# A hybrid attention and state-space layer: the first column blocks turned by diagonal products, a seventh accumulator, joined convolution taps, closing products in one order

## The chip, the cores and the metric

The kernel runs on one NeuronCore of one Trainium2 chip. The metric is device time in microseconds (us) of one execution; the kernel before takes 942.23 us, the median of three runs.

## The reference

One layer over 512 latent tokens and 256 context tokens of width 1024. Both are root-mean-square normalised row by row, shifted and scaled by modulation vectors, and multiplied by one input projection. Its columns feed a low-rank attention with 16 heads, a state-space scan over `x`, `B` and `C` after a depthwise convolution of width 5, and a gate `z`. An output projection, a second modulated norm and a gated feed-forward layer of inner width 2816 follow. Cut to what the change touches:

```python
hx = modulate(rms_norm(x, mix_pre_norm), mod_x[0], mod_x[1])       # 512 x 1024
cq_x, ckv_x, kr_x, z_x, xbc_x, dt_x = in_split(hx @ w_in)
hc = modulate(rms_norm(ctx, mix_pre_norm), mod_c[0], mod_c[1])     # 256 x 1024
xbc = silu(depthwise_conv(xbc, conv_w, conv_b))                    # latent and context apart
ssd = rms_norm(y * silu(z), norm_w)
x = x + mod_x[2] * rms_norm(concat([attn, ssd]) @ w_out, mix_post_norm)
ffn = (gelu(depthwise_conv(gate)) * val) @ w_down
x = x + mod_x[5] * rms_norm(ffn, ffn_post_norm)
```

Everything is float32.

## The kernel before, in words

**How a product is made.** Each operand is split into a high part in float32r and the remainder (`split`: ScalarE copies the high part, VectorE subtracts). A product is three float32r matmuls: high by high, high by low, low by high. Tiles are 128 rows; the 1024 columns are 8 blocks of 128, counted by `k`.

**The start.** SyncE loads four row tiles of `x` (`xn`), two modulation columns and the parameters, then for each `k` the 128 rows of the `z` weights (two halves of 512 columns) and two more modulation columns. PE first runs products of zeros (`IDLE`, 22 of them), then eight small products that spread the vector `c` over all partitions into PSUM (`spread`), then 20 more products of zeros. `unit_rows` squares and sums each row on ScalarE, makes 1/root on VectorE and GpSimd (`rsqrt`: a power on GpSimd, then one Newton step on VectorE), and multiplies each 1024-wide row tile by it (odd tiles on ScalarE, even ones on VectorE); it is called once for tiles 0 and 1 and once for tiles 2 and 3. `columns_of` turns two column blocks of two row tiles by four PE transposes into one PSUM bank, and ScalarE copies them out. `moddot` makes one modulation column by a 1024-wide dot product on VectorE; `factors` makes shift and scale from two of them; `modulated` writes the high part `hx[k]` and the full value on ScalarE, and VectorE makes the low part. Then `part_of_z` multiplies.

**z.** There are eight output tiles of 128 tokens by 512 columns, numbered `n`: 0 to 3 are the first half of the columns, 4 to 7 the second. Each needs a PSUM bank while it sums over `k`. Tiles 0 to 3 hold banks 0 to 3 from `k` = 0. Banks 4 and 5 serve `columns_of`, 6 the products of zeros, 7 is kept free (`m`); tiles 4 to 7 get these four (line 855).

**The x, B and C blocks.** `xbc(m)` makes one block of 128 channels: 24 products over the latent tokens into columns 0 to 511 of a two-bank piece, 24 over the context into columns 512 to 767, then the convolution: ScalarE writes the middle tap with the bias, and VectorE adds the four other taps, once for the latent and once for the context columns.

**The closing.** The down projection is made of seven half-size products in two `series`. The first sums eight accumulators (`n` = 0 to 3, `i` = 0 and 1), the second six (`n` = 0 to 2). In each, the last few `k` of every accumulator (3 and 4 of them) are kept back, and `pins` make the accumulators close one after the other in a given order. After each one `done` adds it to sums on VectorE; an accumulator of the second series needs the sums of the first (`summed_last` reads `u3`, `u2`, `p1`), and when a row tile is whole, `last` normalises it, adds `x` and stores it.

**What sets the order.** The program is written once in plain order; `plan` then orders every engine's instructions by a list scheduler with its own costs (`price`), seeded by `SEED`, with `pins` as extra dependences. Where the instructions of an engine stand is therefore a result of all costs together. All recorded instructions carry the line L137 in the profile, so groups are read by their tiles: `banks` is PSUM, `block` any SBUF tile, `smalls` the per-row scalars.

## Time and profile before

| what | value |
|---|---|
| median of three runs | 942.23 us (941.97 to 942.94) |
| the profiled execution's own time | 942.26 us |
| its span, first to last instruction | 940.5 us |
| PE busy | 917.8 us |
| VectorE (DVE) busy | 808.0 us |
| ScalarE (ACT) busy | 558.6 us |
| GpSimd (POOL) busy | 244.6 us |
| mean granted TensorE clock | 0.992 |

The span plus 1.76 us is the profiled execution's time, and that time is 0.03 us above the median. A row of the timeline gives the start, the length, the engine, the operation with its tiles and shape, and in brackets how long the engine stood idle before it and what ended that. A row of a table by stretch gives the length of the stretch, then for each engine the busy time and the number of instructions, the granted clock, the DMA share and the GB/s. Some matmul records are missing from the trace, so time per product is better taken from starts over a known count.

### The profile page before, as it was taken

The page shows a single profiled execution, that of the slowest core. Times are in us where ns is not written, and L with a number is a line of the kernel's source. Part 1 is how long each engine was busy: PE and PEld are TensorE (multiplying, and loading weights), DVE is VectorE, ACT ScalarE, POOL GpSimd, SP SyncE. Part 2 cuts the span into 40 slices and gives each one's busy share as a digit, 9 for nine tenths or more (in the row PEclk, how much of TensorE's full clock was granted, in tenths as well). Part 3 has the DMA queues.
Part 4 walks back from the last instruction along what each step waited for, and adds up shares of the span by engine and source line. Part 5 has one row for each costly group of instructions (what it writes and reads, how often), then busy time and mean ns, then how long its engine had stood idle before and what let it go on. Part 6 is the DMA issues. An engine that isn't in the chain of part 4 may idle for free.

```text
span 940.5 us, 15221 instructions
## 1 busy us (share of the span) xinstructions
PE 917.8 (98%) x5382; PEld 793.5 (84%) x5382; DVE 808.0 (86%) x1362; ACT 558.6 (59%) x1091; POOL 244.6 (26%) x240
## 2 busy tenths in 40 slices
PE   7999999999999999999999999999999999999994
PEld 6888888788778887988888888899999998888883
DVE  5899887759888988789999828799999899999976
ACT  7667535375668798887875317654454454556631
POOL 1000200847684643610000001600000355330200
PEclk8999999999999999999999999999999999999998
DMA  9999101011521450566639527315243235358732
GB/s 364 348 372 357 35 34 46 7 52 40 122 65 35 125 151 25 157 184 173 197 137 355 187 106 238 121 68 174 73 135 113 68 135 170 124 189 275 194 113 90
DMA packets 51068, 139.97 MB, mean 149 GB/s; under 512 B 8608, under 2 KB 11632, under 8 KB 50992
## 3 DMA queue, kind: packets, MB, share of 16 engines
q1 hardware_dynamic: 48448, 137.85, 44.7%
q10 hardware_dynamic: 2544, 1.15, 0.5%
q8 instruction: 42, 0.69, 0.3%
q14 instruction: 34, 0.28, 0.1%
HBM read 113.90 MB, written 9.35 MB: 131 GB/s over the span
## 4 chain that ended last, share of the span: by engine, by line
PE 84%; DVE 6%; ACT 3%; issue 3%; DMA 2%; POOL 1%; DVEq 0%; POOLq 0%; SPq 0%; ACTq 0%
PE banks L137 84%; DVE block L137 5%; ACT block L137 3%; DVE smalls L137 2%; DMA block<-block 1%; POOL smalls L137 1%; DMA block<-shares 1%; DMA block<-in_xn_dram 1%; POOL block L137 0%; DVEq L1867 0%; POOLq L1867 0%; SPq L137 0%; ACTq L137 0%; DVEq L137 0%; DVE mod L137 0%
## 5 line engine op out<-in xcount | busy, mean ns | idle before, releaser
L137 PE MATMUL banks<-block,block 128*128 128x512 f32 (+2 forms) x4662 | 867.8, 344 | 4.0 <-DVE block L137 1.4
L137 PEld LDWEIGHTS banks<-block,block 128*128 128x128 f32 x4662 | 713.3, 189 | 109.6 <-issue 12.8
L137 DVE TENSOR_TENSOR block<-block,block 128x512 fp32r<-128x512 f32 (+7 forms) x459 | 351.0, 800 | 43.5 <-PE banks L137 16.7
L137 ACT ACTIVATE block<-block 128x512 fp32r<-128x512 f32 (+9 forms) x399 | 267.6, 707 | 202.3 <-DVE block L137 121.5
L137 POOL TENSOR_TENSOR block<-block,block 128x512 f32<-128x512 f32 (+2 forms) x145 | 176.1, 1231 | 312.4 <-DVE block L137 138.5
L137 DVE TENSOR_TENSOR block<-banks,block 128x512 f32<-128x512 f32 (+5 forms) x287 | 168.4, 609 | 33.8 <-PE banks L137 19.1
L137 ACT ACTIVATE block<-banks 128x512 fp32r<-128x512 f32 (+6 forms) x276 | 135.9, 514 | 77.1 <-PE banks L137 68.5
L137 POOL TENSOR_TENSOR block<-block 128x256 f32<-128x256 f32 (+1 forms) x51 | 48.4, 953 | 187.5 <-PE banks L137 132.4
L137 PE MATMUL banks<-cst,block 128*128 128x128 f32 x562 | 89.0, 276 | 3.5 <-DVE block L137 1.8
L137 DVE SCALAR_TENSOR_TENSOR block<-block,block 128x1024 f32<-128x1024 f32 (+2 forms) x74 | 86.9, 1190 | 2.4 <-ACT block L137 1.6
L137 PEld LDWEIGHTS banks<-cst,block 128*128 128x128 f32 x562 | 68.4, 142 | 19.4 <-issue 4.2
L137 ACT ACTIVATE block<-banks,smalls 128x768 f32<-128x768 f32 x64 | 58.0, 907 | 21.2 <-DVE smalls L137 20.5
L137 DVE TENSOR_REDUCE smalls<-banks 128x1 f32<-128x768 f32 x64 | 60.7, 949 | 7.8 <-PE banks L137 6.3
L137 DVE SCALAR_TENSOR_TENSOR block<-banks,cwh,block 128x510 f32<-128x510 f32 (+3 forms) x88 | 52.0, 621 | 7.5 <-ACT block L137 6.9
L137 POOL TENSOR_TENSOR smalls<-smalls,powers 128x1 f32<-128x1 f32 (+3 forms) x17 | 13.0, 767 | 165.1 <-DVE smalls L137 165.1
L137 ACT ACTIVATE block<-banks,block 128x128 f32<-128x128 f32 x128 | 42.2, 382 | 10.7 <-PE banks L137 10.4
L137 ACT ACTIVATE block<-banks,cbh,cwh 128x512 f32<-128x512 f32 (+1 forms) x22 | 14.8, 684 | 26.4 <-PE banks L137 25.6
L137 DVE TENSOR_TENSOR block<-block 128x512 f32<-128x512 f32 (+2 forms) x30 | 20.2, 675 | 1.7 <-DMA block<-in_wup_dram 1.5
L137 ACT ACTIVATE block<-banks,prm 128x512 f32<-128x512 f32 x18 | 13.3, 738 | 9.1 <-PE banks L137 8.1
L137 DVE TENSOR_SCALAR smalls<-smalls 128x1 f32<-128x1 f32 (+3 forms) x36 | 5.9, 170 | 13.1 <-ACT block L137 12.8
L137 ACT ACTIVATE block<-block,prm 128x512 f32<-128x512 f32 x12 | 9.8, 814 | 11.8 <-DVE block L137 11.8
L137 ACT ACTIVATE block<-block,mod,sx 128x512 fp32r<-128x512 f32 (+1 forms) x16 | 13.1, 817 | 4.5 <-DVE sx L137 4.2
(72 smaller groups left out, 234.2 us busy)
## 6 DMA issues: line engine op xcount, KB each, us to landing
block<-in_wmod_dram SPq DMA_DIRECT2D x64, 512.0 KB
block<-in_wup_dram SPq DMA_DIRECT2D x44, 512.0 KB
block<-in_wdn_dram SPq DMA_DIRECT2D x22, 512.0 KB
block<-block SPq DMA_DIRECT2D x32, 256.0 KB
block<-in_wout_dram SPq DMA_DIRECT2D x16, 512.0 KB
block<-block SPq DMA_DIRECT2D x56, 128.0 KB
block<-in_wxbc_dram SPq DMA_DIRECT2D x12, 512.0 KB
block<-in_xn_dram SPq DMA_DIRECT2D x8, 512.0 KB
```

Source lines behind the costliest of these rows:

```text
L137: f(*map(real, args), **{k: real(v) for k, v in kw.items()})
```

## The change

1. **Turning.** For the first two column blocks (`k` = 0 and 1), `columns_of` no longer transposes scaled rows. It multiplies the unscaled block by a 128 by 128 diagonal of 1/root, which turns and scales at once; the diagonals are made on VectorE. The rows are scaled later (`scaled_rows`), for the other blocks. The two modulation columns of `k` = 0 are written ahead of the second pair of rows, and `modulated` works in two halves of 256 tokens for `k` = 0 and 1.
2. **Products of zeros.** The second lot is 34 instead of 20.
3. **Banks.** `spread` uses banks 6 and 7, `columns_of` one bank (4) instead of two; z tiles 4, 5 and 6 hold banks 5, 6 and 7 from `k` = 0, and the eighth tile takes bank 4 at the end.
4. **Taps.** In `xbc` the context columns start at 514, two columns of zeros (written by ScalarE into PSUM) lie between, and each tap is one operation over latent and context columns.
5. **Closing.** `series` returns its last closing, and the second series' first closing is pinned behind the first series' last one.
6. **Planner and loads.** `SEED` is 4 instead of 2, a GpSimd operation on under 8 elements is priced at 550 ns, and the constants are loaded first on SyncE's queue instead of second on ScalarE's. `Calls` records source lines, which changes no instruction.

```diff
-SEED = 2
+SEED = 4
-IDLE = 22, 20
+IDLE = 22, 34
+FM = 2
...
+    if e == "Pool" and n < 8:
+        return 550
...
-    bk.cut(a=[two(0), two(2)], b=[bank(4), bank(5)], s=[bank(6)], m=[bank(7)])
+    bk.cut(a=[two(0), two(2)], b=[bank(4)], s=[bank(5)], v=[two(6)])
...
-    load(cst, a["cst"][:, : P + 32], nc.scalar)
+    load(cst, a["cst"][:, : P + 32])
...
-    def columns_of(pair, k, to):
+    def columns_of(pair, k, to, turn=None):
...
+                if turn is None:
+                    nc.tensor.transpose(o, src, ident)
+                else:
+                    mm(o, lhsT=src, rhs=turn[:, i * P : (i + 1) * P], start=True, stop=True)
...
-    unit_rows(xn[:2])
-    unit_rows(xn[2:])
+    turns = []
+    for h in range(2):
+        pair, turn = xn[2 * h : 2 * h + 2], t2(P, 256)
+        r = unit_rows(pair)
+        for i in range(2):
+            V.tensor_scalar(out=turn[:, i * P : (i + 1) * P], in0=ident, scalar1=r[:, i : i + 1], scalar2=None, op0=ALU.mult)
+        columns_of(pair, 0, xT[0][:, :, h * 256 : h * 256 + 256], turn)
+        turns.append(r)
+        if not h:
+            scaled_rows(pair, r)
+            for j in (0, KD)[:FM]:
+                moddot(wmods[j], pv, mod[:, j : j + 1])
...
+        if k == 1:
+            scaled_rows(xn[2:], turns[1])
-        if k % 2 == 0:
+        if k and k % 2 == 0:
...
+            bk.cut(v=[], s=[bank(5), bank(6), bank(7)])
+            zp += [pget("s") for _ in range(3)]
...
+    zp.append(pget("b"))
...
+        n = CO + CT if m < 10 else S
+        if m < 10:
+            act(pm[:, S:CO], none, AF.Copy)
+        gemm_T(blk(w), KD, ((pm[:, :S], hxv), (pm[:, CO:n], hcv))[: 2 if m < 10 else 1])
+        st = t4(P, n)
+        act(st, pm[:, :n], AF.Identity, scale=cwh[:, m * 5 + 2 : m * 5 + 3], bias=cbh[:, m : m + 1])
...
-    def series(terms, banks, keep, done, order):
+    def series(terms, banks, keep, done, order, after=None):
...
-        at = []
+        at = [after] if after else []
...
+        return at[-1]
...
-    series(rest_of_right, banks(3), 4, summed_last, [(n, i) for n in range(3) for i in range(2)])
+    series(rest_of_right, banks(3), 4, summed_last, [(n, i) for n in range(3) for i in range(2)], first_done)
```

**Where instructions move.** PE at the start of the program, before. `128x256` are the products of zeros, `sel` the spread, `cst` the identity of a transpose, `block_2` to `block_5` the row tiles 0 to 3, `128x512` the first products of z.

```order
L137 MATMUL banks<-block_1_87 128x256 x22
L137 MATMUL banks<-block_1_87,sel 128x128 x8
L137 MATMUL banks<-block_1_87 128x256 x19
L137 MATMUL banks<-cst,block_2_85 128x128
...
L137 MATMUL banks<-cst,block_4_98 128x128
L137 MATMUL banks<-cst,block_5_107 128x128
...
L137 MATMUL banks<-block_1_87,block_20_231 128x512
```

The same place after the change; `block_16_175` and `block_21_224` are the diagonals of the two pairs of row tiles.

```order
L688 MATMUL banks<-block_1_87 128x256 x22
L688 MATMUL banks<-block_1_87,sel 128x128 x8
L688 MATMUL banks<-block_1_87 128x256 x21
L688 MATMUL banks<-block_16_175,block_2_91 128x128
...
L688 MATMUL banks<-block_1_87 128x256 x13
L688 MATMUL banks<-block_21_224,block_4_101 128x128
...
L688 MATMUL banks<-block_1_87,block_24_222 128x512 x2
```

Before, 20 transposes (column blocks 0 to 3 of tiles 0 and 1, then blocks 0 and 1 and so on) stand ahead of the first product of z and 12 between its first products; after, 8 products by diagonals stand ahead of it, with 13 products of zeros between the first four and the last four, and the 24 other transposes stand among the products of z, in sixes of four.

VectorE at the same place, before: `block_2_85` and `block_4_98` are row tiles 0 and 2, `block_6` and `block_7` the modulation columns.

```order
L137 SCALAR_TENSOR_TENSOR smalls<-smalls 128x2
L137 TENSOR_SCALAR block_2_85<-block_2_85,smalls 128x1024
L137 TENSOR_SCALAR smalls<-smalls 128x2 x2
L137 TENSOR_TENSOR smalls<-smalls 128x2 x2
...
L137 TENSOR_SCALAR block_4_98<-block_4_98,smalls 128x1024
L137 SCALAR_TENSOR_TENSOR block_16_125,mod<-block_6_119,banks 128x1024
L137 SCALAR_TENSOR_TENSOR block_22_211,mod<-block_7_131,banks 128x1024
L137 TENSOR_TENSOR mod<-mod,prm 128x2
L137 SCALAR_TENSOR_TENSOR sx<-mod,prm 128x1
```

After, from the first pair's 1/root on.

```order
L688 TENSOR_SCALAR block_16_175<-cst,smalls 128x128 x2
L688 TENSOR_SCALAR block_2_91<-block_2_91,smalls 128x1024
L688 SCALAR_TENSOR_TENSOR block_19_195,mod<-block_6_124,banks 128x1024
L688 TENSOR_SCALAR smalls<-smalls 128x2
L688 SCALAR_TENSOR_TENSOR block_20_208,mod<-block_7_134,banks 128x1024
...
L688 TENSOR_TENSOR smalls<-smalls 128x2
L688 TENSOR_TENSOR mod<-mod,prm 128x2
...
L688 SCALAR_TENSOR_TENSOR sx<-mod,prm 128x1
L688 SCALAR_TENSOR_TENSOR smalls<-smalls 128x2
L688 TENSOR_SCALAR block_21_224<-cst,smalls 128x128 x2
```

The two dot products now stand ahead of the second pair's 1/root, and the second pair's diagonals come after `sx`, the scale factor of `k` = 0.

PE at the end of the program, before: the last products. `block_1236` and `block_1240` are left operands of the first series, `block_1478` and `block_1488` of the second; each group of three rows is one `k` of one accumulator.

```order
L137 MATMUL banks<-block_1511_8571,block_1236_7788 128x512
L137 MATMUL banks<-block_464_2860,block_1236_7788 128x512
L137 MATMUL banks<-block_1511_8571,block_1237_7813 128x512
L137 MATMUL banks<-block_1100_6748,block_1240_7697 128x512
L137 MATMUL banks<-block_1401_8620,block_1240_7697 128x512
L137 MATMUL banks<-block_1100_6748,block_599_3821 128x512
L137 MATMUL banks<-block_880_5489,block_1478_8450 128x512
L137 MATMUL banks<-block_1115_6787,block_1478_8450 128x512
L137 MATMUL banks<-block_880_5489,block_1479_8539 128x512
L137 MATMUL banks<-block_1494_8478,block_1488_8493 128x512
```

After: the last ten rows of PE. `block_1480`, `block_827` (its low part `block_1491`), `block_1234` and `block_1432` are left operands of the second series.

```order
L688 MATMUL banks<-block_1486_8543,block_885_5521 128x512
L688 MATMUL banks<-block_1364_8279,block_827_4122 128x512 x2
L688 MATMUL banks<-block_1364_8279,block_1491_8509 128x512
L688 MATMUL banks<-block_1506_8548,block_1234_7711 128x512
L688 MATMUL banks<-block_1266_7801,block_1234_7711 128x512
L688 MATMUL banks<-block_1506_8548,block_1501_8563 128x512
L688 MATMUL banks<-block_1464_8448,block_1432_8296 128x512
L688 MATMUL banks<-block_1445_8488,block_1432_8296 128x512
L688 MATMUL banks<-block_1464_8448,block_1511_8571 128x512
```

By the banks that the products write, the first series' last two accumulators (`n` = 3) close 26 and 12 products ahead of PE's last product before, and 204 and 162 ahead of it after. The second series' six accumulators close 77, 65, 53, 41, 21 and 0 products ahead of PE's last one before, and 83, 71, 59, 36, 12 and 0 after.

In counts, PE has 14 more products of zeros and 8 products by a diagonal in place of 8 transposes; VectorE has 40 taps in place of 80 for the ten joined blocks; ScalarE has ten two-column writes more and six table loads instead of four, all of the two extra among the x, B and C blocks.

More of the change, by code (lines that the diff above doesn't have):

```diff
@@ L4 @@
 import random
+import sys
 from contextlib import ExitStack
@@ L135, in make @@
         for i in order:
-            f, args, kw = self.calls[i]
-            f(*map(real, args), **{k: real(v) for k, v in kw.items()})
+            f, args, kw, line = self.calls[i]
+            if line not in self.at:
+                self.at[line] = compile("\n" * (line - 1) + "f(*args, **kw)", __file__, "exec")
+            exec(self.at[line], dict(f=f, args=list(map(real, args)), kw={k: real(v) for k, v in kw.items()}))
 class Memory:
@@ L781, in factors, with modulated @@
                                op0=ALU.add, op1=ALU.mult)
[L783 to L786 removed]
+    def modulated(k, xk, md, aa, hi, lo, cuts=1):
+        w = xk.shape[1] // cuts
+        for h in (slice(o, o + w) for o in range(0, w * cuts, w)):
+            for to in (hi, xk):
+                act(to[:, h], xk[:, h], AF.Identity, scale=aa[:, k : k + 1], bias=md[:, k : k + 1])
+            V.tensor_tensor(out=lo[:, h], in0=xk[:, h], in1=hi[:, h], op=ALU.subtract)
     warm, pw = t2(dt=F32R), pget("s")
@@ L847, in build @@
             pfree(pv)
-        for nh in range(2):
-            wz[nh, k] = weight(a["wz"][k][:, nh * 512 : nh * 512 + 512], 512)
         urgent.append(((mark, here()),))
@@ L863, in build @@
         dump(f"hx{k}", hx[k].rearrange("p a b -> p (a b)"))
-    pfree(*za, *zp[NX:])
-    pv = spread(1)
+    pfree(*za)
+    pv = spread(1, "a")
     act(csc, pv, AF.Copy)
-    pfree(pv)
+    pfree(pv, *zp[NX:])
+    bk.cut(b=[bank(4), bank(5)], s=[])
     cn = [t4() for _ in range(2)]
@@ L881, in build @@
         modulated(k, ctt[k // 4][:, k % 4, :], modc, scx, hcp[k // 2][:, k % 2, 0, :], hcp[k // 2][:, k % 2, 1, :])
-    bk.cut(a=[two(0), two(2)], b=[bank(4), bank(5)], s=[bank(6), bank(7)], m=[])
+    bk.cut(a=[two(0), two(2)], b=[bank(4), bank(5)], s=[bank(6), bank(7)])
     def gemm_T(wf, nk, cols, parts=((0, 0), (0, 1), (1, 0))):
@@ L909, in build @@
     xs, bn, bct = [None] * 2, [None] * 2, [None] * 2
+    CO = S + 2
+    none = c_([P, 2], "none")
+    G.memset(none, 0.0)
     def xbc(m):
@@ L1793, in build @@
     banks = lambda n: [[pget("a") for _ in range(2)] for _ in range(n)]
-    series(sums_of_right, banks(4), 3, summed_first, [(n, i) for n in range(4) for i in range(2)])
+    first_done = series(sums_of_right, banks(4), 3, summed_first, [(n, i) for n in range(4) for i in range(2)])
     def summed_last(n, i, po):
```

60 lines of the change are left out of this document (27 added, 33 removed).

## The prediction

> **What bounds the kernel now.** I read the page's busy times first, then the stretches, then the chain of waits and the timeline at both ends.
>
> ```profile
> PE 917.8 (98%) x5382; PEld 793.5 (84%) x5382; DVE 808.0 (86%) x1362; ACT 558.6 (59%) x1091; POOL 244.6 (26%) x240
> 0.00:20.00 20.00, 15.29 (x75) 12.66 (x75) 10.17 (x27) 14.95 (x24) 2.81 (x13) 0.83 0.92 356
> 40.00:60.00 20.00, 20.00 (x94) 16.70 (x93) 19.07 (x42) 14.92 (x23) 1.60 (x1) 1.00 0.98 375
> 160.00:200.00 40.00, 40.00 (x211) 31.52 (x210) 34.18 (x66) 19.32 (x42) 25.01 (x23) 1.00 0.03 10
> 300.00:350.00 50.00, 49.56 (x316) 42.06 (x315) 44.97 (x83) 43.54 (x121) 27.88 (x31) 1.00 0.47 126
> 400.00:450.00 50.00, 48.06 (x315) 42.15 (x314) 44.43 (x69) 39.16 (x80) 5.87 (x4) 1.00 0.68 182
> 450.00:500.00 50.00, 49.21 (x332) 43.00 (x333) 48.39 (x79) 38.37 (x81) 2.59 (x2) 1.00 0.54 176
> 550.00:600.00 50.00, 49.55 (x278) 43.16 (x276) 35.61 (x74) 28.51 (x58) 12.00 (x13) 1.00 0.58 189
> 600.00:700.00 100.00, 98.83 (x734) 94.38 (x735) 94.77 (x140) 50.19 (x70) 8.84 (x4) 1.00 0.31 106
> ```
>
> PE is the bound: full in the rows of 40 and 160, with idle of 0.44, 1.94, 0.79, 0.45 and 1.17 us in the rows from 300 on, 4.8 us in all. The number of products of the layer stays. So time can only come from three places: before PE runs full, those gaps, and what follows PE's last product. VectorE, ScalarE or queue time in between is worth nothing unless PE waits for it.
>
> **The end.** PE's last products, then what VectorE and the queue do after them (a table of stretches, then the timeline):
>
> ```profile
> 914.40:921.40 7.00, 7.00 (x32) 5.79 (x32) 0.04 (x1) 0.07 (x1) 0.00 (x0) 1.00 0.00 0
> 921.40:927.30 5.90, 5.89 (x27) 4.54 (x25) 5.85 (x12) 2.52 (x7) 1.07 (x2) 1.00 0.00 0
> 927.30:940.50 13.20, 0.00 (x0) 0.00 (x0) 9.65 (x27) 1.53 (x6) 1.10 (x2) 0.66 0.41 160
> 850.00:900.00 50.00, 50.00 (x223) 41.40 (x222) 47.67 (x82) 34.90 (x66) 6.21 (x1) 1.00 0.69 204
> 899.45 9.52 DVE L137 TENSOR_TENSOR block<-block,block 128x512 fp32r<-128x512 f32 x17 [0.47 <-PE banks L137]
> 921.44 2.48 DVE L137 TENSOR_TENSOR block<-banks,block 128x512 f32<-128x512 f32 x4 [7.00 <-PE banks L137]
> 926.76 0.63 ACT L137 ACTIVATE block<-block 128x512 f32<-128x512 f32 x1 [2.02 <-DVE block L137]
> 927.30 0.19 ACT L137 ACTIVATION_READ_ACCUMULATOR block<-block 128x1 f32 x1
> 927.78 0.68 DVE L137 TENSOR_TENSOR block<-banks,block 128x512 f32<-128x512 f32 x1
> 930.57 0.74 DVE L137 SCALAR_TENSOR_TENSOR block<-block,smalls,block 128x512 f32<-128x512 f32 x1
> 935.82 1.40 DVE L137 SCALAR_TENSOR_TENSOR block<-block,smalls,block 128x512 f32<-128x512 f32 x2
> ```
>
> VectorE stands idle for 7.00 us while PE works, is then full from 921.4 to 937.2 (935.82 + 1.40), 9.9 us past PE's end at 927.3, and the last store takes 3.3 us more. The reason is the order of closing. An accumulator of the second series is added to sums of the first series' `n` = 3, and those two close 26 and 12 products from the end; so nearly all sums, all four normalisations and all stores queue up behind them.
>
> After the change these two close 204 and 162 products from the end, and the second series' last three at 36, 12 and 0. At 0.21 us a product (20 us over the 94 of the row 40 to 60) they lie 7.7, 2.6 and 0 us before the end. VectorE then has left, after PE's last product: its sum 0.68 (after 0.25 us of waiting, my estimate), a scaling of the other row 0.74, the product with the gate 0.69, a small step 0.17, a scaling 0.69, two small steps and the Newton step 0.5, two scalings 1.40: 5.1 us. The square (0.63 + 0.19) and the power on GpSimd lie beside scalings of the other row. So VectorE ends 5.1 us past PE instead of 9.9: **minus 4.8 us**. Of VectorE's work, 5.5 us (eight operations of 0.69) are moved ahead of the last operand splits, which end at 908.97 before, 18.3 us ahead of PE's end; they then end 12.8 us ahead, and the order leaves 12 operations of 0.69 and 11 small ones of 0.17, 10.2 us of VectorE work, between them and PE's end. That fits, by 2.6 us. If it doesn't, PE or the tail slips: bounds minus 3.0 and minus 5.5 (the small steps hidden too).
>
> **The start.** The chain of waits runs through the second pair of rows; timeline and stretches:
>
> ```profile
> 9.08 1.16 ACT L137 ACTIVATE block<-block,smalls 128x1024 f32<-128x1024 f32 x1 [0.32 <-DVE smalls L137]
> 10.14 1.04 ACT L137 ACTIVATE block<-block 128x1024 f32<-128x1024 f32 x1
> 8.88 0.16 DVE L137 SCALAR_TENSOR_TENSOR smalls<-smalls 128x2 f32<-128x2 f32 x1
> 9.08 0.76 DVE L137 TENSOR_SCALAR block<-block,smalls 128x1024 f32<-128x1024 f32 x1
> 13.55 1.21 DVE L137 SCALAR_TENSOR_TENSOR block<-block,banks 128x1024 f32<-128x1024 f32 x1
> 14.00 1.14 ACT L137 ACTIVATE block<-block 128x512 fp32r<-128x512 f32 x2
> 13.69 1.36 PE L137 MATMUL banks<-cst,block 128*128 128x128 f32 x4 [1.23 <-DVE block L137]
> 17.84 2.50 PE L137 MATMUL banks<-block,block 128*128 128x512 f32 x5
> 20.22 1.14 PE L137 MATMUL banks<-cst,block 128*128 128x128 f32 x8
> 21.11 3.26 PE L137 MATMUL banks<-block,block 128*128 128x512 f32 x13
> 11.00:12.00 1.00, 0.19 (x2) 0.19 (x3) 0.34 (x2) 0.76 (x3) 0.45 (x1) 1.00 1.07 402
> 12.00:13.00 1.00, 0.47 (x4) 0.23 (x3) 0.60 (x4) 0.06 (x1) 0.26 (x1) 1.00 1.06 428
> 13.00:14.00 1.00, 0.31 (x1) 0.18 (x1) 1.00 (x2) 1.00 (x2) 0.00 (x0) 0.70 1.04 426
> 19.00:20.00 1.00, 1.00 (x4) 0.48 (x2) 1.00 (x2) 1.00 (x3) 0.00 (x0) 0.50 1.10 428
> L137 DVE CAST sel<-cst 128x32 fp32r<-128x32 f32 x1 | 0.2, 181 | 1.0 <-DMA cst<-in_cst_dram 1.0
> L137 PE MATMUL banks<-block 128*128 128x128 f32 x16 | 2.1, 275 | 0.0
> ```
>
> The scaling of row tile 1 holds the last square back on ScalarE (9.08 to 10.14), and the two dot products start only at 13.55, after the second pair's rows; the first product of z starts at 17.84.
>
> After the change, 1/root of the first pair is there at 9.05 (8.88 + 0.16), plus 0.3 us because the constants are now issued ahead of `x` on SyncE's queue (an estimate): 9.35. Two diagonals at 0.2 (nearest: the 128x32 cast, 0.18) to 9.75, one row scaled to 10.5, two dot products of 1.22 with a small step between to 13.1, six small steps to 14.1, two diagonals to 14.5. Four products by the second diagonal, at 0.26 each (2.1 us over the 16 records of the eight other full float32 products of that size), and a wait of 0.15: the first product of z at 15.7, 2.1 us sooner. Against it: 24 transposes remain instead of 12, at 0.11 (eight start within 0.89 us), plus 1.3 us. For it: from about 13.4 (0.70 in the row of 13) to 20.2 the granted clock was 0.50, and five products of z took 2.38 us from start to start instead of 1.07; with 13 more products of zeros in the rows of 11 and 12, where PE was 0.19 and 0.47 busy, I take the clock as full, minus 1.3 us. Against it again: ScalarE. Between the first copy (11.5 to 12.1) and the first half's high part stand a scaling of 1.16 and two splits of 0.57, then the copy of `c`, so the second pair's copy ends about 17.2; as only one bank serves the turning, each of the next five groups of transposes waits for the copy before it, at its place in PE's order. I count waits of 0.2 to 0.4 us there, 1.7 in all. The sum: minus 2.1, plus 1.3, minus 1.3, plus 1.7: **minus 0.4 us**. Bounds: minus 2.1 if the waits vanish, plus 1.3 if the clock falls all the same.
>
> [...]
>
> The seventh accumulator gives PE more products per `k`, but PE starves nowhere in the row of 40, so it counts nothing; what it covers is the transposes that now stand among the products.
>
> **The taps.**
>
> ```profile
> L137 DVE SCALAR_TENSOR_TENSOR block<-banks,cwh,block 128x511 f32<-128x511 f32 x24 | 17.9, 744 | 0.3
> L137 DVE SCALAR_TENSOR_TENSOR block<-banks,cwh,block 128x255 f32<-128x255 f32 x20 | 9.4, 474 | 0.1
> L137 ACT ACT_TABLE_LOAD x4 | 5.1, 1283 | 2.4 <-PEq L1863 1.7 <-DVE block L137 0.7
> L137 ACT ACTIVATE hd<-hd 128x32 f32<-128x32 f32 x1 | 0.2, 216 | 0.0
> ```
>
> A pair of taps cost 0.744 + 0.474 = 1.22 us; 769 columns cost 0.744 + 258 x 0.00105 = 1.01. Forty times 0.21 is 8.4 us off VectorE, all of it where PE is full (row 160 to 200): **nothing**. The ten two-column writes (0.22 each, by the smallest activation) and two more table loads (2.6 us) go to ScalarE, which is half busy there. A write ends the wait for a PSUM piece, and PE's product over the context waits for it; but the plan puts 12 or more latent products of the same block, 2.6 us, ahead of the first context product. Without that cover it would be 0.22 plus what stands ahead on ScalarE.
>
> **The rest of the order** is drawn anew, with another seed and a truer price for the power on GpSimd. The five gaps can close (minus 4.8) or grow. Nothing in the trace says which; I take **nothing**, with 1.5 us either way.
>
> **Sum.** 942.26 - 4.8 - 0.4 = 937.06: **937.0 us**, for the median too, which is 0.03 us below the profiled execution.
>
> **Rivals.**
>
> *VectorE is late at the close* (0.10). The 7.00 us of idle are filled and 2.6 us of slack is little: if splits come late, PE waits in its last 24 products and the gain at the end shrinks to about 1.5 us: 942.26 - 1.5 - 0.4 = 940.4. For it: VectorE is 47.67 of 50 us busy from 850 on. Against it: the 7.00 us.
>
> *The whole start comes through* (0.15): no waits for the single bank, clock full: minus 2.1 instead of minus 0.4, so 935.4.
>
> *The new order opens gaps* (0.10): some 4 us more of waits in the attention stage, where 400 to 500 has most of them: about 941.
>
> *The two-column write becomes a wait* (0.06, slower). Bank free by VectorE's last tap, then ScalarE's queue, then PE: if PE stood 0.75 us, one activation, at each of ten blocks, 7.5 us: 944.6. It outweighs the gain from 0.52 us a block. Against it: 2.6 us of latent products ahead.
>
> *The first pair's diagonals save nothing* because `sx` comes as late as before (the dot products wait for their load): start plus 0.5, the rest as forecast: 937.9; it lies within the forecast.
>
> The forecast has 0.59. Range: 934.5 (the better start, and some gap closed) to 940.6 (a late VectorE, or 1.5 us of gaps with half the gain). About 0.2%, 1.9 us, is what a measurement of this kernel can tell from no change. Faster holds the forecast, the better start and 0.03 of two rivals each: 0.80; same 0.14; slower 0.06.
>
> **What would show it.** Right: VectorE's idle stretch of 7 us before the end is gone and it ends about 5 us after PE's last product; the first product of z near 15.7 at clock 1.00; taps of 769 columns near 1.0 us. Wrong: a clock of 0.50 between 13 and 20 us; PE idle by VectorE in its last 15 us; PE waiting for ScalarE among the x, B and C blocks; PE idle above 6 us between 300 and 602.

## The result, and the profile after

The changed kernel takes 934.42 us (median of six runs, 933.71 to 936.12), the kernel before 942.37 in the same comparison (941.67 to 943.73). The ratio is 0.9917, with a 95% interval of 0.9905 to 0.9930: 7.9 us faster where 5.3 were forecast, and 0.1 us below the lower end of the forecast's range, 934.5. The profiled execution took 935.4 us, with a span of 933.6; before, 942.26 and 940.5.

The page's line of busy times of the changed kernel:

```profile
PE 915.1 (98%) x5404; PEld 793.5 (85%) x5404; DVE 806.2 (86%) x1328; ACT 558.8 (60%) x1097; POOL 245.7 (26%) x241
```

VectorE is busy for 1.8 us less in all, though the taps alone take some 8 us off it. The four diagonals give 1.0 us back. Much of the rest is the same operations taking longer: 16 casts of 128x256 take 8.7 us instead of 4.2, eight operations of 128x128 that read `cst` 6.3 instead of 3.5. The runs do not show why. Stretches of the changed kernel (length, then busy time and count of PE, weight loads, VectorE, ScalarE, GpSimd, the granted clock, DMA share, GB/s):

```profile
12.00:20.00 8.00, 5.68 (x35) 4.93 (x35) 7.38 (x21) 7.45 (x12) 0.71 (x1) 1.00 1.03 401
300.00:615.00 315.00, 311.49 (x1930) 271.84 (x1930) 266.95 (x461) 218.83 (x479) 81.22 (x79) 1.00 0.55 163
914.40:921.40 7.00, 7.00 (x32) 5.82 (x31) 6.39 (x16) 1.45 (x4) 0.92 (x1) 1.00 0.39 150
923.87:933.60 9.73, 0.00 (x0) 0.00 (x0) 4.66 (x11) 0.72 (x2) 0.99 (x1) 0.62 0.28 109
```

The stretch 914.4 to 921.4, in which VectorE did 0.04 us of work before, now holds 6.39 us of it. The clock is 1.00 from 12 to 20 us; before, it was at 0.50 from 13.4 to 20.2. The stretch 300 to 615 before, for comparison:

```profile
300.00:615.00 315.00, 310.19 (x1894) 267.77 (x1893) 261.02 (x458) 217.11 (x474) 85.68 (x82) 1.00 0.53 163
```

PE idles 1.3 us less there and starts 36 more products in the same 315 us.

The end, in the timeline (start, length, engine, operation, in brackets the idle time before it and what ended that):

```profile
889.71 34.16 PE L688 MATMUL banks<-block,block 128*128 128x512 f32 x150
921.26 0.69 DVE L688 TENSOR_TENSOR block<-banks,block 128x512 f32<-128x512 f32 x1 [0.50 <-PE banks L688]
927.57 1.41 DVE L688 SCALAR_TENSOR_TENSOR block<-block,smalls,block 128x512 f32<-128x512 f32 x2
```

PE ends at 923.87 (889.71 + 34.16), VectorE at 928.98: 5.1 us later instead of 9.9. The span ends 4.6 us after VectorE; before it was 3.3.

**A measure of PE's loss.** PE is busy in nearly every row, so busy time does not show where it gained. I take instead, at a time t, all products that have not begun, each at the median start-to-start time of its shape and operands over all kernels below (0.227 us for 128x512, 0.12 for 128x256, 0.109 for a transpose), and add their sum to t. That is where PE would end if nothing more were lost; what it grows by from one t to the next is loss, as idle time or as wider spacing. At 60 us it takes in the start. The table has one profiled execution of each kernel (the names are those of the experiments below). Such an execution can lie 1 to 2 us from its kernel's median (plus 1.0 for after, 0.9 for after_twotaps, 1.2 for after_seed3, minus 2.1 for after_best, within 0.4 for the others), so a difference of 1 or 2 us between two rows of one column is not much by itself.

| kernel | time, us | ratio to before (95%) | PE's end as seen at 60 us | lost 60 to 300 | 300 to 615 | 615 to PE's end | VectorE past PE | span past VectorE |
|---|---|---|---|---|---|---|---|---|
| before | 942.4 | 1 | 883.1 | 17.5 | 26.4 | 0.4 | 9.9 | 3.3 |
| after | 934.4 | 0.9917 (0.9905 to 0.9930) | 882.4 | 17.8 | 23.3 | 0.3 | 5.1 | 4.6 |
| before_pin | 937.1 | 0.9951 (0.9939 to 0.9963) | 883.2 | 18.9 | 24.1 | 0.7 | 5.4 | 3.0 |
| before_seed4 | 941.8 | 0.9987 (0.9978 to 0.9995) | 884.5 | 18.4 | 24.2 | 0.4 | 9.6 | 3.1 |
| after_nopin | 939.7 | 0.9986 (0.9965 to 1.0007) | 882.8 | 19.0 | 21.4 | 1.0 | 10.4 | 3.1 |
| after_zeros20 | 937.3 | 0.9952 (0.9940 to 0.9963) | 884.9 | 18.4 | 23.1 | 0.3 | 5.1 | 3.8 |
| after_scaled | 938.1 | 0.9950 (0.9936 to 0.9964) | 883.6 | 18.4 | 22.7 | 2.7 | 5.1 | 3.8 |
| after_twotaps | 937.1 | 0.9938 (0.9924 to 0.9952) | 882.7 | 17.3 | 27.1 | 0.2 | 5.1 | 3.7 |
| after_twotaps_seed2 | 937.1 | 0.9930 (0.9917 to 0.9943) | 883.2 | 18.2 | 25.0 | 0.3 | 5.2 | 3.7 |
| after_seed2 | 932.8 | 0.9900 (0.9888 to 0.9913) | 883.0 | 17.9 | 21.0 | 0.2 | 5.1 | 3.8 |
| after_seed3 | 934.6 | 0.9904 (0.9890 to 0.9918) | 882.6 | 17.7 | 23.4 | 1.3 | 5.2 | 3.8 |
| after_oldprice | 941.8 | 0.9990 (0.9975 to 1.0005) | 884.6 | 23.1 | 20.3 | 3.9 | 5.4 | 3.1 |
| after_oldprice_seed2 | 935.3 | 0.9913 (0.9902 to 0.9925) | 885.0 | 18.8 | 20.6 | 0.3 | 5.7 | 3.1 |
| after_best | 937.6 | 0.9933 (0.9919 to 0.9948) | 882.1 | 19.4 | 23.1 | 0.2 | 4.8 | 3.8 |

The five columns on the right and the one at 60 us add up to a span. Between the spans of before and after: start minus 0.7, 60 us to PE's end minus 2.7, VectorE past PE minus 4.8, the last store plus 1.3; in all minus 6.9. The kernels ran on different chips, with 942.3 to 943.3 us for the kernel before, so kernels are compared by their ratios.

### The profile page after: what moved, and what is told of

It reads as the page before. It is cut to its first block, busy times and chain, and to the rows that moved or that the text cites. A ratio compares the mean times of both kernels' runs of the same rounds, so it can differ in the third digit from the quotient of the medians.

```text
span 933.6 us, 15216 instructions
## 1 busy us (share of the span) xinstructions
PE 915.1 (98%) x5404; PEld 793.5 (85%) x5404; DVE 806.2 (86%) x1328; ACT 558.8 (60%) x1097; POOL 245.7 (26%) x241
## 3 DMA queue, kind: packets, MB, share of 16 engines
HBM read 113.90 MB, written 9.35 MB: 132 GB/s over the span
## 4 chain that ended last, share of the span: by engine, by line
PE 86%; DVE 7%; ACT 2%; issue 2%; DMA 2%; SPq 0%; POOLq 0%; DVEq 0%; POOL 0%; ACTq 0%
PE banks L688 86%; DVE block L688 6%; ACT block L688 2%; DMA block<-in_wz_dram 1%; DVE smalls L688 1%; DMA block<-block 1%; SPq L688 0%; POOLq L1903 0%; DVE mod L688 0%; DVEq L1903 0%; DVE sx L688 0%; POOL smalls L688 0%; ACT banks L688 0%; ACTq L688 0%; DVEq L688 0%
## 5 line engine op out<-in xcount | busy, mean ns | idle before, releaser
L688 PEld LDWEIGHTS banks<-block,block 128*128 128x128 f32 x4678 | 713.8, 189 | 112.7 <-issue 15.7
L688 ACT ACTIVATE block<-block 128x512 fp32r<-128x512 f32 (+7 forms) x399 | 267.1, 706 | 188.5 <-DVE block L688 124.9
L688 DVE TENSOR_TENSOR block<-block,block 128x512 fp32r<-128x512 f32 (+8 forms) x461 | 349.7, 796 | 28.3 <-ACT block L688 13.4
L688 DVE TENSOR_TENSOR block<-banks,block 128x256 fp32r<-128x256 f32 (+5 forms) x287 | 170.2, 610 | 37.5 <-ACT block L688 17.9
L688 ACT ACTIVATE block<-banks 128x256 fp32r<-128x256 f32 (+7 forms) x276 | 135.2, 512 | 80.4 <-PE banks L688 69.8
L688 PE MATMUL banks<-cst,block 128*128 128x128 f32 (+1 forms) x554 | 86.6, 272 | 0.1
L688 PEld LDWEIGHTS banks<-cst,block 128*128 128x128 f32 (+1 forms) x554 | 66.6, 140 | 13.4 <-issue 2.1
L688 POOL TENSOR_TENSOR smalls<-smalls,powers 128x1 f32<-128x1 f32 (+3 forms) x17 | 13.4, 787 | 160.4 <-DVE smalls L688 153.6
L688 ACT ACTIVATE block<-banks,block 128x128 f32<-128x128 f32 x128 | 41.7, 376 | 14.1 <-PE banks L688 13.5
L688 DVE SCALAR_TENSOR_TENSOR block<-banks,cwh,block 128x768 f32<-128x768 f32 (+3 forms) x48 | 46.6, 970 | 3.7 <-ACT block L688 2.8
L688 DVE TENSOR_TENSOR block<-block 128x512 f32<-128x512 f32 (+1 forms) x30 | 19.9, 667 | 0.3 <-PE banks L688 0.2
L688 ACT ACTIVATE block<-banks,cbh,cwh 128x770 f32<-128x770 f32 (+1 forms) x12 | 11.5, 955 | 11.4 <-PE banks L688 11.4
L688 ACT ACTIVATE block<-block,mod,sx 128x512 fp32r<-128x512 f32 (+3 forms) x20 | 14.5, 728 | 1.9 <-DVE sx L688 1.4
```

The costliest lines, as they stand in the source:

```text
L688: G.memset(powers, -0.5)
```

## The experiments

Every edit makes the planner draw the whole order anew; each is therefore read by its part of the table first, and by its time second.

**The pin alone, on the kernel before** (before_pin).

```diff
-    def series(terms, banks, keep, done, order):
+    def series(terms, banks, keep, done, order, after=None):
...
-        at = []
+        at = [after] if after else []
...
+        return at[-1]
```

> The kernel before, with the closing pin alone (the last three products are held in order and behind the first four). Theory (the pin is what shortened the end): VectorE ends about 5.1 us past PE's last product instead of 9.9, the span ends 9.7 to 11 us past PE's last product instead of 13.2, and the time is 938.9 us (942.4 less 3.5), 937.4 to 940.4 since the order in the middle is drawn anew with any edit. Rival (the end came from the new draw or from the new price of small GpSimd operations): VectorE still ends 9 us or more past PE and the time stays 941 to 944.

Measured 937.11 us. The stretch behind PE's last product:

```profile
926.91:935.30 8.39, 0.01 (x1) 0.00 (x0) 4.78 (x11) 0.72 (x2) 0.55 (x1) 0.65 0.33 126
```

VectorE's last two operations, in the timeline:

```profile
930.89 1.41 DVE L137 SCALAR_TENSOR_TENSOR block<-block,smalls,block 128x512 f32<-128x512 f32 x2
```

VectorE has 4.78 us left instead of 9.65 and ends at 932.30, 5.4 us past PE. The span ends 8.4 us past PE instead of 13.2 (9.7 to 11 were expected), and the time lies 0.3 us below its range. The gain is 0.49%, 4.6 us; in the profiled executions 4.8 of 5.2 us are the shorter end. The rival falls.

**The changed kernel without the pin** (after_nopin).

```diff
-    series(rest_of_right, banks(3), 4, summed_last, [(n, i) for n in range(3) for i in range(2)], first_done)
+    series(rest_of_right, banks(3), 4, summed_last, [(n, i) for n in range(3) for i in range(2)])
```

> The changed kernel without the closing pin. Theory: the 7 us of idle VectorE just before the close comes back, VectorE ends 9 to 10 us past PE's last product, and the time is 937.9 us (934.4 and 3.5), 936.4 to 939.4. Rival (the pin does nothing of its own): VectorE still ends about 5 us past PE, and the time is 934.4, 933 to 936.

Measured 939.73 us. Two stretches near the end:

```profile
914.40:921.40 7.00, 7.00 (x33) 5.79 (x32) 2.49 (x5) 0.72 (x2) 0.00 (x0) 1.00 0.00 0
924.26:937.80 13.54, 0.00 (x0) 0.00 (x0) 10.19 (x29) 1.79 (x6) 1.61 (x3) 0.59 0.41 156
```

The first of VectorE's sums of the close, in the timeline, with the idle time ahead of it:

```profile
918.91 1.29 DVE L688 TENSOR_TENSOR block<-banks,block 128x512 f32<-128x512 f32 x2 [7.42 <-PE banks L688]
```

The idle stretch is back (7.42 us) and VectorE works 10.19 us behind PE. PE's end is within 0.4 us of the changed kernel's, so the mechanism is as forecast. VectorE's lateness (10.4 us) and the time lie a little above what was expected. The time rose by 0.69%, 6.5 us, instead of 3.5. Two of the twelve executions took 947.3 and 947.6 us, all others 937.8 to 940.2, and they raise the ratio; between the two medians it is 5.3 us. Of the rest, 1.0 us is the expectation's own: it took the end from one execution of the changed kernel, which lay 1.0 us over its median and had a late store (below).

This run also shows the clock. At the start its PE does the same products in the same order as the changed kernel's. Its timeline:

```profile
15.08 4.11 PE L688 MATMUL banks<-block,block 128*128 128x128 f32 x14 [2.33 <-ACT block L688]
19.03 0.60 PE L688 MATMUL banks<-cst,block 128*128 128x128 f32 x4
```

Its clock in the stretch between, in the last column but two:

```profile
16.00:18.00 2.00, 2.00 (x9) 1.71 (x8) 1.37 (x3) 1.79 (x3) 0.00 (x0) 0.50 1.04 402
```

And the timeline of the changed kernel, whose clock is 1.00 there:

```profile
15.39 2.52 PE L688 MATMUL banks<-block,block 128*128 128x128 f32 x14 [2.32 <-ACT block L688]
17.75 0.60 PE L688 MATMUL banks<-cst,block 128*128 128x128 f32 x4
```

At clock 0.50 the same 14 products take 3.95 us to the next transposes instead of 2.36, 1.6 us more. They began 0.31 us sooner, so the transposes are 1.28 us late; the prediction gave the clock 1.3. So the 34 zeros alone did not keep it: it stayed at 1.00 in the execution of the changed kernel that was profiled, and not here. At 60 us PE's end is seen 0.4 us later than in the changed kernel.

**20 products of zeros instead of 34** (after_zeros20).

```diff
-IDLE = 22, 34
+IDLE = 22, 20
```

> The changed kernel with 20 zero products instead of 34 behind the spread, so that the 13 between the two pairs of rows go. TensorE then stands idle for about 4 us ahead of its first z product, in place of 1.3 and 2.3. Theory (the zeros keep the clock full): the granted clock falls to 0.50 somewhere between 13 and 20 us, as in the kernel before, and that costs about 1.3 us: 935.7, 934.2 to 937.2 with the order drawn anew. Rival (the zeros do nothing, the clock stays at 1.00 without them): every window up to 25 us at 1.00, and 934.4, 933 to 936.

Measured 937.28 us. Stretches of the start:

```profile
12.00:14.00 2.00, 0.00 (x0) 0.00 (x0) 2.00 (x4) 1.55 (x3) 0.70 (x1) 0.53 1.06 408
14.00:16.00 2.00, 0.81 (x4) 0.84 (x5) 1.85 (x12) 1.97 (x5) 0.00 (x0) 0.50 1.01 396
16.00:18.00 2.00, 2.00 (x9) 1.45 (x9) 2.00 (x3) 1.56 (x3) 0.00 (x0) 0.50 1.05 402
18.00:20.00 2.00, 2.00 (x10) 1.82 (x10) 1.97 (x8) 1.97 (x3) 0.00 (x0) 0.76 1.02 399
```

PE's first group behind the idle time, in the timeline:

```profile
15.20 2.90 PE L688 MATMUL banks<-block,block 128*128 128x128 f32 x10 [3.88 <-ACT block L688]
```

PE idles 3.88 us and the clock is at 0.50 from 12.1 to 19.0 us. PE's end as seen at 60 us is 2.5 us later than in the changed kernel, and the time follows (plus 0.35%, 3.3 us), two and a half times what was expected and 0.1 us over the range. The rival falls; that the zeros are worth this much by the clock alone does not follow, as an idle stretch of 0.52 us at 22.5 us and a different order of work came with it.

**Another draw of the changed kernel** (after_seed2).

```diff
-SEED = 4
+SEED = 2
```

> The changed kernel with the seed of the kernel before: nothing but the planner's draw of the order differs. Theory (the 2.6 us won in the middle, between the first blocks and the close, are the luck of a draw): the start and the end stay (the end 9.7 us from PE's last product, clock full), the middle moves by 1 to 3 us either way: 934 to 937.5, likeliest 936. Rival (the middle's gain is the changed work itself, above all the 8 us off VectorE): the middle stays within 0.5 us, and the time is 934.4, within 0.6.

Measured 932.75 us, faster than the changed kernel and outside both expectations. The stretch 300 to 615:

```profile
300.00:615.00 315.00, 313.10 (x1942) 273.12 (x1940) 270.98 (x466) 221.95 (x484) 85.71 (x84) 1.00 0.55 165
```

It idles 1.6 us less there than the changed kernel and starts 12 more products. The loss behind 60 us is 39.1 instead of 41.4, so a draw does move the middle by over 2 us. But the two kernels with the old work so far lost 44.2 and 43.7, and the four with the new 39.1 to 41.7: that the middle's gain is luck alone became less likely, and the next runs ask which part of the work it is.

**Old taps, new everything else** (after_twotaps).

```diff
-        gemm_T(blk(w), KD, ((pm[:, :S], hxv), (pm[:, CO:n], hcv))[: 2 if m < 10 else 1])
-        st = t4(P, n)
+        gemm_T(blk(w), KD, both(pm) if m < 10 else ((pm[:, :S], hxv),))
+        st = t4(P, T)
+        for o, n in ((0, S), (S, CT))[: 2 if m < 10 else 1]:
...
+                lo, hi = o + max(0, -d), o + n - max(0, d)
```

> The changed kernel with the old taps: latent and context columns in separate operations, no two zero columns. So far PE lost 44.2 and 43.7 us between 60 us and its last product in the two kernels with the old work (against its products at their median spacing) and 41.4, 41.4, 41.7 and 39.1 us in the four with the new. Theory A (the taps gave the middle's 2.5 us, by taking 8.4 us off VectorE): the loss goes back to 43.5 to 44.5 and the time to 937, 936 to 938.5. Theory B (the taps are hidden, as forecast): the loss stays at 41 to 42 and the time at 934.4, 933.4 to 936.

Measured 937.06 us; the ratio rose from 0.9917 to 0.9938 (0.9924 to 0.9952), 2.0 us, with intervals that overlap by a little. The stretch 300 to 615:

```profile
300.00:615.00 315.00, 310.06 (x1893) 267.15 (x1892) 269.70 (x459) 216.25 (x474) 82.55 (x81) 1.00 0.53 164
```

The loss behind 60 us is 44.6, 0.1 over theory A's range, and the time lies within it. But the loss is not where the taps are. They run from about 55 to 245 us, and from 60 to 300 the old taps lose 17.3 us, the joined ones 17.8. All of the difference lies behind 300 us: 1893 products begun instead of 1930.

**The old price of small GpSimd operations** (after_oldprice).

```diff
-    if e == "Pool" and n < 8:
-        return 550
```

> The changed kernel without the planner's price of 550 ns for GpSimd operations under 8 columns; no operation differs, only the planned order can. Theory A (the taps gave the middle): the loss behind 60 us stays at 41 to 42 us, time 934.4, 933.4 to 936. Theory B (the truer price gave the middle, by an order with fewer waits): the loss goes to 43.5 to 44.5, time 937, 936 to 938.5. In both the end keeps its 5 us from PE's last product to VectorE's last.

Measured 941.83 us, 7 us slower and beyond both. The stretch 60 to 130:

```profile
60.00:130.00 70.00, 67.87 (x339) 57.27 (x338) 60.22 (x106) 36.81 (x58) 8.40 (x5) 0.98 0.54 196
```

PE's longest wait in it, in the timeline:

```profile
102.83 1.05 PE L686 MATMUL banks<-ones,block 128*128 128x1 f32 x8 [1.78 <-POOL block L686]
```

The same stretch of the changed kernel:

```profile
60.00:130.00 70.00, 70.00 (x371) 59.79 (x370) 66.94 (x112) 44.58 (x70) 3.92 (x3) 1.00 0.60 218
```

PE waits 1.78 us for GpSimd. Behind that wait the clock is at 0.50 once more, from 105.1 to 108.5. In the stretch 32 fewer products begin. Another 3.9 us go behind 615 us, 2.1 of them in four waits for VectorE and ScalarE between 869 and 906. From 300 to 615, however, this kernel is the best of all (20.3).

**The seed of the changed kernel, on the kernel before** (before_seed4).

```diff
-SEED = 2
+SEED = 4
```

> The kernel before with the seed of the changed one, nothing else. Theory (the middle's gain belongs to the changed work or the price, a seed moves it by about 2 us either way): PE's loss behind 60 us 42.5 to 46 us, VectorE still 9 to 10 us late at the close, time 942.3, 940.5 to 944.5. Rival (the seed gave the middle's gain): the loss falls to about 41.5 and the time to 939.7, 939 to 940.5.

Measured 941.82 us. The stretch 300 to 615:

```profile
300.00:615.00 315.00, 311.02 (x1911) 269.60 (x1910) 264.66 (x462) 217.48 (x477) 86.53 (x80) 1.00 0.53 162
```

The loss behind 60 us is 43.0, and VectorE ends 9.6 us past PE. The seed gives 1.2 us at most; the rival falls.

**The first two blocks turned as before** (after_scaled).

```diff
-        pair, turn = xn[2 * h : 2 * h + 2], t2(P, 256)
-        r = unit_rows(pair)
-        for i in range(2):
-            V.tensor_scalar(out=turn[:, i * P : (i + 1) * P], in0=ident, scalar1=r[:, i : i + 1], scalar2=None, op0=ALU.mult)
-        columns_of(pair, 0, xT[0][:, :, h * 256 : h * 256 + 256], turn)
-        turns.append(r)
+        pair = xn[2 * h : 2 * h + 2]
+        scaled_rows(pair, unit_rows(pair))
+        columns_of(pair, 0, xT[0][:, :, h * 256 : h * 256 + 256])
```

> The changed kernel with the first two blocks turned as before: rows scaled first, then transposed; the seven accumulators, the 34 zeros, the taps and the pin stay. Theory (the diagonals bring the first product of z forward by about 1.4 us, and with the rest of the start 0.6 us at 60 us): first product of z at 17 to 18 us instead of 16.3, PE's projected end at 60 us later by 0.5 to 1.5, time 935.4, 934.4 to 937. Rival (the diagonals save nothing that lasts, their full products and the 12 more transposes eat it): projected end at 60 us within 0.3, time 934.4, 933.4 to 935.4.

Measured 938.09 us. PE at the start, and one of two waits near the end:

```profile
15.16 0.91 PE L688 MATMUL banks<-cst,block 128*128 128x128 f32 x4 [2.84 <-DVE block L688]
16.01 0.98 PE L688 MATMUL banks<-block,block 128*128 128x512 f32 x3
...
907.12 20.28 PE L688 MATMUL banks<-block,block 128*128 128x512 f32 x88 [0.74 <-DVE block L688]
```

The first product of z starts at 16.01, no later than in the changed kernel (16.28): that expectation was wrong. But only three follow before the next transposes, and at 60 us PE's end is seen 1.2 us later than in the changed kernel, 0.8 later than in after_nopin, whose clock fell for as long. So the diagonals are worth about 1 us at 60 us (an estimate, with another order of work in each kernel), though the first product gains nothing. The time is 3.1 us over the changed kernel's by the ratios and 1.1 us over the expected range: another 2.4 us were lost behind 615 us, 1.7 of them in two waits for VectorE, at 879 and 906.

**Old taps with the other seed** (after_twotaps_seed2: the two edits of after_twotaps and after_seed2 together).

> The old taps once more (latent and context columns apart), with the seed of the kernel before in place of the changed one's: with seed 2 the joined taps lost 39.1 us behind 60 us and took 932.75 us. Theory A (the joined taps are worth the 2.6 to 3 us of the first such run, whatever the draw): loss 41.5 to 42.5, time 935.5, 934.7 to 936.5. Theory B (the taps are hidden, and the first run drew a worse order): loss anywhere between 39 and 44, a mean of the two pairs within 1.5 us of nothing; a time under 934.3 speaks for B.

Measured 937.12 us, and the stretch 300 to 615:

```profile
300.00:615.00 315.00, 310.60 (x1900) 268.50 (x1899) 267.15 (x457) 215.31 (x472) 82.44 (x81) 1.00 0.52 163
```

The loss is 43.4 where joined taps had 39.1, and the ratio is 0.9930 (0.9917 to 0.9943) against 0.9900 (0.9888 to 0.9913): 2.8 us, with intervals that do not meet. The two pairs give 2.4 us on the mean, more than the 1.5 that theory B allowed, so B falls by its own sign. Theory A's numbers did not come either: the loss and the time are 0.9 and 0.6 us over its ranges. Over the table, the five kernels with old taps lose 24.1 to 27.1 us from 300 to 615, the nine with joined taps 20.3 to 23.4, whatever their seed, price, start and end.

That makes a gain by the joined taps likely, and the prediction's zero with it likely wrong. It is not shown as cleanly as the end is. Two seeds are two draws; after_best below, with joined taps, loses as much behind 60 us (42.7) as kernels with old ones; and the stretch was chosen after the runs. How operations that end at 245 us shorten the stretch behind 300 was not isolated either. Steps of over 0.6 us beyond the median cost 4.2 us there with old taps and 2.4 with joined ones, as means of the five and the nine (3.3 to 5.4 and 0.8 to 4.3), all shorter ones 21.1 and 19.7. The nearest candidate would be work that VectorE still has to do at 300 us. In the two pairs its busy time behind 300 us is 4.1 and 2.2 us less with joined taps, but over all fourteen kernels it does not tell the two groups apart: 562.0 to 570.0 us with old taps, 561.3 to 575.7 with joined ones.

**The old price with the other seed** (after_oldprice_seed2: the edits of after_oldprice and after_seed2).

> The old price of small GpSimd operations once more, with seed 2. With seed 4 the old price cost 7.4 us: 5.9 in the loss behind 60 us (47.3 instead of 41.4), the rest before 60 us. Theory A (the price itself is worth several us, as orders planned without it wait for GpSimd): loss over 43, time 936.5 to 940. Theory B (a bad draw, the price is worth little): loss 39 to 42, time 932.5 to 935.5.

Measured 935.33 us, loss 39.7. Against after_seed2 the price is worth 0.13%, 1.2 us, with intervals that overlap by a little, and not 7. Theory B holds for the loss behind 60 us. What stays with both seeds is the start: seen at 60 us, PE's end is 884.6 and 885.0 with the old price and 882.4 and 883.0 with the new.

**A third draw** (after_seed3: seed 3).

> The changed kernel with a third seed, for the spread of draws. If a draw moves the middle by a standard deviation of about 1.7 us, as the five kernels with joined taps and new price so far (39.1, 41.4, 41.4, 41.7 and 43.8): loss 39 to 44, time 932.5 to 937.5, likeliest 934.5. If the changed work and price set the middle: loss 39 to 42, time 932.5 to 935.3. The end keeps its 5 us from PE's last product to VectorE's last in both.

Measured 934.57 us, loss 42.5: between the draws, and the end as always. Against their own runs of before, the three seeds of the changed kernel give 0.9917, 0.9900 and 0.9904.

**More zeros and another queue for the last store** (after_best).

```diff
-SEED = 4
+SEED = 2
...
-IDLE = 22, 34
+IDLE = 22, 46
...
-            load(out[i * P : (i + 1) * P, h], res[i][:, h])
+            load(out[i * P : (i + 1) * P, h], res[i][:, h], nc.scalar if i == 1 and h.start else None)
```

> The changed kernel with seed 2, with 46 zero products instead of 34 behind the spread, and with the very last store issued by ScalarE's queue instead of SyncE's. Zeros: 12 more at 0.14 us fill 1.6 of the 2.3 us in which TensorE waited for ScalarE; every window of 3.41 us then holds more than 2.4 us of work, and the clock should stay at 1.00 (seed 2 had 0.50 for 3.41 us); gain 0.6 to 1.1 us at 30 us. If they are in the way instead, the first product of z comes later than 16 us. Store: if the two last stores wait for one another on SyncE's queue, the span ends 3.0 to 3.4 us past VectorE's last instruction instead of 3.8, a gain of 0.4 to 0.8; if the time is the transfer's own, 3.8 stays. With both: 931.4; with neither 932.75; and 1.7 us either way for the order drawn anew.

Measured 937.58 us: 3.1 us slower than after_seed2 by the ratios, and over everything that was expected. PE at the start, in the timeline:

```profile
11.17 3.23 PE L688 MATMUL banks<-block 128*128 128x256 f32 x25
15.29 2.52 PE L688 MATMUL banks<-block,block 128*128 128x128 f32 x14 [0.89 <-ACT block L688]
```

The stretch behind PE's last product:

```profile
924.79:933.30 8.51, 0.00 (x0) 0.00 (x0) 4.66 (x11) 0.72 (x2) 0.55 (x1) 0.76 0.32 123
```

The 25 zeros fill most of the wait (0.89 us are left of 2.3), the first product of z comes no later for it, the clock stays at 1.00, and PE's end as seen at 60 us is the earliest of all: 0.9 us ahead of after_seed2, as expected. This order then loses 3.7 us more than after_seed2's from 60 us on, in an execution 2.1 us under the kernel's median. With the same seed and the same taps, an order drawn anew can therefore cost as much as the taps seem to be worth. The store's queue changes nothing: the span ends 3.8 us past VectorE with either. That theory falls, and the next section says what it is instead. The fastest version is after_seed2; with its stores issued in the order of their data it might gain 0.7 us more (an estimate from one store of 256 KB, below), which was not tried.

## Why the prediction was right or wrong

**The end, minus 4.8: right in mechanism and size.** VectorE ends 5.1 us past PE, as the sum of eight steps had it, and two runs that put the pin in and take it out move this number between 5.1 or 5.4 and 9.9 or 10.4.

**"The last store takes 3.3 us more": wrong by 1.3 us.** The step kept the store's cost of before. SyncE issues stores in a planned order, and it is another one now. The last four on its queue, as they stand in the changed program:

```
L688 DMA out_dram<-block_1251_8700 128x512
L688 DMA out_dram<-block_1252_8719 128x512
L688 DMA out_dram<-block_1251_8700 128x512
L688 DMA out_dram<-block_1252_8719 128x512
```

The second half of one row tile stands behind the first half of the next. Its data is there at 926.68 (925.94 + 0.74), the first half's at about 928.3, the middle of the second row below:

```profile
925.94 0.74 DVE L688 SCALAR_TENSOR_TENSOR block<-block,smalls,block 128x512 f32<-128x512 f32 x1
927.57 1.41 DVE L688 SCALAR_TENSOR_TENSOR block<-block,smalls,block 128x512 f32<-128x512 f32 x2
...
928.35 0.33 SPq L688 DMA_DIRECT2D out_dram<-block  x1
...
929.46 0.39 SPq L688 DMA_DIRECT2D out_dram<-block  x1
```

No store is issued between 925.65 (the one before these, 925.32 and 0.33) and 928.35, and then three leave within 1.1 us (the second at 929.02). Three stores of 256 KB at about 390 GB/s, the rate in the rows of GB/s below, take 2.0 us, two take 1.3 (an estimate). In the six kernels whose stores go out 0.03 us after their data, the span ends 3.0 to 3.3 us past VectorE; in seven others with a store held back, 3.7 to 3.8. The changed kernel's own 4.6 has something more, in the GB/s of its last stretch (927.0 to 933.6, in 40 slices), beside those of after_seed2 (925 to 931):

```profile
GB/s 0 0 0 0 0 0 0 0 0 0 0 0 0 273 385 397 348 373 397 335 385 385 372 372 397 298 37 25 25 12 0 0 0 0 0 0 0 0 0 0
```

```profile
GB/s 82 0 0 0 0 0 0 0 0 0 0 0 0 0 0 96 396 369 355 410 369 382 369 396 410 369 369 382 423 151 0 0 0 0 0 0 0 0 0 0
```

For four slices at the end, 0.66 us, it moves 12 to 37 GB/s, 25 on the mean, beside 24 for one of the 16 DMA engines that the page counts (a sixteenth of 390). The last store lands 2.87 us behind its issue, in after_seed2 2.50. So about 0.4 of the extra 0.8 us is this slow end of the transfer; another 0.2 lie ahead of the last issue and 0.2 behind the landing. Why they differ in this execution the trace does not say.

**The start, minus 0.4: right in sum, by errors that cancel.** PE at the start of the changed kernel, and the two steps on VectorE that the prediction named:

```profile
10.36 1.16 PE L688 MATMUL banks<-block,block 128*128 128x128 f32 x8 [1.29 <-DVE block L688]
11.28 1.80 PE L688 MATMUL banks<-block 128*128 128x256 f32 x13
...
18.11 5.76 PE L688 MATMUL banks<-block,block 128*128 128x512 f32 x24
...
13.22 1.21 DVE L688 SCALAR_TENSOR_TENSOR block<-block,banks 128x1024 f32<-128x1024 f32 x1
14.69 0.15 DVE L688 SCALAR_TENSOR_TENSOR sx<-mod,prm 128x1 f32<-128x1 f32 x1
```

The first product of z (a record within the group at 15.39) starts at 16.28, not 15.7. The roots of the first pair come at 9.99 and not 9.35, and VectorE then waits 0.83 us for PE before it scales the row, so the second dot product ends at 14.43 and not 13.1; shorter small steps (0.6 us from there to the second diagonals, where 1.0 was forecast) and quicker products by the diagonal (0.22 us each from start to start, not 0.26) win back all but 0.6 us. The waits of 1.7 us for the single bank did not come; PE never idles between 15.4 and 40 us. The transposes (0.09 us each, plus 1.1 for the twelve more where 1.3 was forecast) and the clock (1.00, minus 1.3) are about as forecast in this execution. Together that is about minus 1.6 us at 30 us (PE's end as seen there is 881.4 instead of 883.0), of which 0.7 is left at 60 us. That the clock's term came true in this execution is luck in part: of the nine kernels with 34 zeros the profiled clock stayed at 1.00 in two and fell to 0.50 for 3.41 us in seven, after_nopin among them. The four kernels with 20 zeros all had 0.50 for 6.83 us, so on these records the zeros shorten the fall more often than they keep it away. With 46, in after_best, there was none.

**The taps, nothing: likely wrong, and then the largest miss.** Of the 6.9 us between the two spans, 2.7 came between 60 us and PE's end, where the prediction had nothing, with 1.5 us either way. The price of an operation was right:

```profile
L688 DVE SCALAR_TENSOR_TENSOR block<-banks,cwh,block 128x769 f32<-128x769 f32 x20 | 20.3, 1015 | 0.5
...
L688 ACT ACTIVATE banks<-none 128x2 f32<-128x2 f32 x10 | 1.7, 172 | 19.3 <-DVE block L688 19.0 <-PE banks L688 0.3
```

It is 1.015 us against 1.01. Nor did the two-column write become a wait: 0.17 us each, and PE waits for ScalarE 3.6 us in all, of which 2.3 are at the start. What failed, as far as the runs show it, is the step from "PE is full where the taps run" to "nothing": the gain, 2.0 us with one seed and 2.8 with the other, shows in a later stretch. One reading is that PE's full rows hide what the other engines still owe when PE begins to depend on them, and that the planner moves this debt. No run shows that: VectorE's busy time behind 300 us agrees in the two pairs and not over all kernels, so the path from the taps to the later stretch stays open.

**The rest of the order, nothing with 1.5 us either way: too narrow.** Three seeds of the changed kernel span 1.6 us, two of the kernel before 1.2, and that fits. But an order drawn anew by a small edit cost more: 3.1 us in after_best against after_seed2, and with the old price 7 us with one seed and 1.2 with the other. So some luck of the draw in the missing 2.6 us is not ruled out; the two pairs with old taps only make it unlikely to be all of it.

None of the rivals came true. VectorE is not late at the close, and the whole start came through only as far as 30 us.

## What to carry to other kernels

An operation that is hidden where it runs may still be worth something later (here the joined taps' 2.0 and 2.8 us showed behind 300 us, by a path that no run shows): ask what the freed engine will have done by the next stretch in which PE waits. The end of this kernel is a chain over several queues, and the order of the stores on theirs belongs to the sum as VectorE's steps do: in the seven kernels above with a store held back the span ended 3.7 to 3.8 us past VectorE instead of 3.0 to 3.3. Where a planner draws the order anew, compare a part of the change with several seeds (two were few here), and read the parts of the span rather than its length alone.

## What was not expected of the hardware

**The clock changes in steps of 3.41 us.** In all 14 profiled executions the granted clock stays at one level for a multiple of 3.413 us, counted from its rise: before, 6.83 us at 1.00, 6.83 at 0.50 and 911.36 at 1.00 (2, 2 and 267 times 3.413), in the changed kernel 921.60 us at 1.00 (270 times). Where it falls at the start, it is at 0.50 for 3.41 or 6.83 us. The rise lies anywhere from 4.2 to 7.5 us after the first instruction (6.57 before, 4.67 in the changed kernel). Cut into stretches of 3.41 us from the rise on, PE's records show 32 to 50% busy in the stretch ahead of each of the 11 falls at the start; the three executions without a fall had no stretch under 61 (after_oldprice_seed2), 59 (after_best) and 46% (the changed kernel). Before, the stretch ahead of the fall at 13.4 us was 44% busy, and PE's longest wait around it lasted 1.23 us. A twelfth fall, at 105.1 us in after_oldprice, came behind a stretch that its records show 67% busy:

```profile
101.72:105.13 3.41, 2.30 (x16) 2.13 (x17) 0.33 (x2) 2.12 (x3) 2.02 (x2) 1.00 0.00 0
```

Half of its 16 products move one column each (eight in 1.05 us); what those count for the clock no run shows. No sharp border comes out of these shares: in one execution the clock fell after 50%, in another it did not after 46%. The gap of 2.33 us in after_nopin lay within one stretch, which was 32% busy, and the clock fell. The border at 14.9 us cut the changed kernel's gap of 2.32 us into 1.84 and 0.48, its stretches were 46 and 86% busy, and the clock stayed. That the place of the border decided between the two is a reading of these two executions; no run isolates it.
